# Two of the four sets of activation sums are formed in a later stage of an encoder block, from a second load of x

## The chip, the cores and the metric

One NeuronCore of a Trainium2 chip runs the whole block as one program. The metric is the device time of one execution in microseconds (us); a figure called a median is the median of three runs. A profiled execution has a time of its own and a trace. Its engines are PE (matrix multiply), PEld (the weight loads of PE), ACT (ScalarE), DVE (VectorE), POOL (GpSimd) and SP (which here only issues DMAs). Times "at" a moment are us from the start of the profiled span.

## The reference, cut to what matters

The input x is 512 tokens by 1024 features in float32. One layer is computed:

```python
h = _rmsnorm(x, g_pre_mix)                 # x * rsqrt(mean(x^2) + eps) * g
proj = h @ w_in                            # 1024 x 7168
q, k, v, g, u, sv, a_ret, a_sgu = jnp.split(proj, ...)   # 512,512,1024,1024,1024,1024,1024,1024
y_ret = _retention_branch(q, k, v, g, ret_decay_logit, w_ret_o)
y_sgu = _sgu_branch(u, sv, ..., w_sgu_o)
merged = jax.nn.sigmoid(a_ret) * y_ret + jax.nn.sigmoid(a_sgu) * y_sgu
x = x + _rmsnorm(merged @ w_out, g_post_mix)
h2 = _rmsnorm(x, g_pre_ffn)
x = x + _rmsnorm(_conv_gated_mlp(h2, w_up, conv_w, conv_b, w_down), g_post_ffn)
```

Retention works on chunks of the sequence with learned decays, forward and backward; its output is normed per head, multiplied by silu(g) (the first of the gates) and projected. The spatial branch multiplies gelu(u) by a mix over 128 positions of the normed gelu(sv).

## The kernel before, in words

**Numbers.** Every float32 operand of a matmul is split into a high and a low part in PE's fast float32 form: ACT copies the value into the high part (`copy`, L71) and DVE subtracts it from the value for the low part (`split`, L76 to L78). A product is then three matmuls: high by high, high by low, low by high.

**Weights.** All weight matrices lie in HBM as 146 blocks of 128 by 1024, in the order of use. `w_get` (L154) loads and splits them some blocks ahead: SP issues the load into one of 4 `raw` tiles, ACT and DVE split it into a ring of 9 `w4` slots. A block's split waits until PE is through with the block whose slot it takes, and its load until the split that used the raw tile before is done.

**Order.** The Python code records the work, and when the program is built a scheduler lays it out as one fixed list for each engine. An engine works strictly down its own list; it waits at the head of it when an operand or a buffer isn't ready. SBUF tiles of 128 by 512 come from a pool of 74 (`blk`), short-lived ones from a ring of 6 (`tmp`). PSUM is a ring of 8 banks (`ps`).

**First stage (L188 to L240): q and k.** x is loaded transposed, as eight tiles `xT` of 128 features by 512 tokens. For each k, `load_x` (L190) loads one, ACT multiplies it by the norm's weight into the high part `xh` (L194), DVE makes the low part `xl` (L200), and `x_scaled` (L204) has ACT write the same product once more in plain float32, `xg` (L207). PE then adds this k's part of 8 outputs, which fill all 8 PSUM banks (`qk`). At the end (L317 to L324) ACT copies the four even banks and DVE the four odd ones to SBUF (`qkraw`).

**The sums of activations.** The projections u, a_ret and a_sgu use a seven-product form of a 2 by 2 block multiplication (`Pair`, L600): the two halves of the tokens (T0, T1) by the two halves of the features (k = 0..3 and 4..7). The blocks of x enter as they are and as four sums S1 to S4. `x_forms(k)` (L248) makes one of four sets of those sums from `xg[k]` and `xg[k + 4]`: four DVE operations on half tiles (L252 to L255), and two splits (two ACT copies `sh`, two DVE subtractions `sl`). The four calls stand at L289, behind the sum of squares of x (ACT, L283, on eight more loads of x; DVE, L286; POOL, L273 and L276), which gives the norm's row scale `rstd`.

**Then.** A small matmul spreads `rstd` over a PSUM bank (L329, `rbc`); rotary and decay of head 0 are prepared (`prep`); and six groups `t_group` (L422) of 4 weight blocks each make v (two), sv (two) and g (two), each into 4 banks, with the retention of one head between them. `t_group` yields after each of its 4 blocks. The last group, the second half of g, stands alone at L584; its evacuation `g_evac` (L563) has ACT apply silu into a `tmp` tile, DVE multiply, and PE transpose (L557). u comes next, and its weights come in seven forms (`w_form`, L131): B11, B21 and B22 as loaded, T1 and T3 added by DVE (L142, L143), T2 and T4 added by POOL (L144, L146). Then come the gates with the output projections, `w_out`, and the gated MLP.

Of the kernel before, what the change touches and what calls it, by code (L numbers as in the profile page):

```python
# [12 lines left out]
AF = mybir.ActivationFunctionType  # L13
# [21 lines left out]
PRE, FFNG, LNG, LNB = 0, 8, 16, 24  # L35
# [5 lines left out]
def tile_block(ctx: ExitStack, tc, xT, x, wall, par, cs, decay, wsp, bsp, gpost, gffn, out):  # L41
    nc = tc.nc
# [5 lines left out]
    def nm(s):  # L48
        uid[0] += 1
        return f"{s}_{uid[0]}"  # L50

    def blk(dt=F32, n="blk", shape=(P, S)):
        return sb.tile(list(shape), dt, tag="blk", bufs=NBLK, name=nm(n))

    def tmp(n="tmp", shape=(P, S)):
        return sb.tile(list(shape), F32, tag="tmp", bufs=6, name=nm(n))
# [7 lines left out]
    def ps(shape=(P, S)):  # L64
        return pp.tile(list(shape), F32, tag="ps", name=nm("ps"))
# [4 lines left out]
    def copy(o, i):  # L70
        nc.scalar.activation(out=o, in_=i, func=AF.Copy)  # L71

    def as32(t):
        return t.bitcast(F32)

    def split(hi, lo, src):  # L76
        copy(hi, src)
        nc.vector.tensor_sub(lo, src, as32(hi))  # L78
# [75 lines left out]
    def w_get(look=LOOK):  # L154

        i = w_pos[0]
        w_pos[0] += 1
        room = 2 * look + (2 if units[i][0] == "blk" else 0)
        n = sum(w_size(u) for u in units[i : w_pos[1]])
        while w_pos[1] < len(units) and (w_pos[1] <= i or n + w_size(units[w_pos[1]]) <= max(room, 9 if look == LOOK else 0)):  # L160
            u = units[w_pos[1]]
            w_ready[w_pos[1]] = w_block(u[1]) if u[0] == "blk" else w_form(*u)
            w_pos[1] += 1
            n += w_size(u)
        return w_ready.pop(i)

    def mm3(o, ah, al, bh, bl, start, stop):
        nc.tensor.matmul(o, ah, bh, start=start, stop=False)  # L168
        nc.tensor.matmul(o, ah, bl, start=False, stop=False)  # L169
        nc.tensor.matmul(o, al, bh, start=False, stop=stop)  # L170
# [14 lines left out]
    def col(i):  # L185
        return part[:, i : i + 1]

    xh, xl, xg = [], [], []  # L188

    def load_x(k):  # L190
        t = tmp("xT")
        nc.sync.dma_start(t, xT[k])
        h_, l_ = blk(F32R, "xh"), blk(F32R, "xl")
        nc.scalar.activation(out=h_, in_=t, func=AF.Copy, scale=col(PRE + k))  # L194
        xh.append(h_)
        xl.append(l_)
        return t

    def x_low(k, t):
        nc.vector.scalar_tensor_tensor(  # L200
            out=xl[k], in0=t, scalar=col(PRE + k), in1=as32(xh[k]), op0=ALU.mult, op1=ALU.subtract
        )

    def x_scaled():  # L204
        k = len(xg)
        xg.append(blk(n="xg"))
        nc.scalar.activation(out=xg[k], in_=xts[k], func=AF.Copy, scale=col(PRE + k))  # L207


    hold = raw_tile()  # L210
# [6 lines left out]
    xts = []  # L217
    for k in range(KD):
        xt = load_x(k)
        xts.append(xt)  # L220
        if k:
            x_low(k, xt)
        if k == 2:
            copy(hold[:, 0:16], as32(xl[1])[:, 0:16])
        wh, wl = w_get(1 if k < 4 else LOOK)
        if k == 0:
            x_low(k, xt)
            for a, b in ((wh, xh), (wl, xh), (wh, xl)):
                for m in range(8):
                    nc.tensor.matmul(  # L230
                        qk[m], a[:, m * P : (m + 1) * P], b[0], start=a is wh and b is xh, stop=False
                    )
            continue
        if k > 1:
            x_scaled()
        for m in range(8):
            c = slice(m * P, (m + 1) * P)
            mm3(qk[m], wh[:, c], wl[:, c], xh[k], xl[k], False, k == KD - 1)
    x_scaled()
    x_scaled()  # L240

# [4 lines left out]
    def x_forms(k):  # L248

        a, b = xg[k], xg[k + 4]  # L250
        s_ = blk(n="xs")
        nc.vector.tensor_sub(s_[:, T0], a[:, T1], b[:, T1])  # L252
        nc.vector.tensor_sub(s_[:, T1], s_[:, T0], a[:, T0])
        nc.vector.tensor_sub(a[:, T0], a[:, T0], a[:, T1])
        nc.vector.tensor_add(a[:, T1], b[:, T0], s_[:, T1])  # L255
        for names, s_ in (("S1", "S2"), s_), (("S3", "S4"), a):
            h_, l_ = blk(F32R, "sh"), blk(F32R, "sl")
            split(h_, l_, s_)
            for n, t in zip(names, (T0, T1)):
                forms[n].append((h_[:, t], l_[:, t]))  # L260
# [9 lines left out]
    def rsqrt(o, v, scale, w):  # L270

        t = small("rs", 16, 4)
        nc.gpsimd.tensor_scalar(  # L273
            out=t[:, :w], in0=v, scalar1=scale, scalar2=EPS, op0=ALU.mult, op1=ALU.add
        )
        nc.gpsimd.tensor_tensor(out=o, in0=t[:, :w], in1=nhalf[:, :w], op=ALU.pow)  # L276

    ss = const("ss", [P, 16])
    for t in range(NT):
        for n in range(2):  # L280
# [3 lines left out]
                out=xt, in_=xt, func=AF.Square, accum_out=ss[:, 4 * n + t : 4 * n + t + 1]  # L284
# [1 line left out]
    nc.vector.tensor_add(ss[:, :NT], ss[:, :NT], ss[:, NT : 2 * NT])  # L286
    rstd = const("rstd", [P, NT])
    rsqrt(rstd, ss[:, :NT], 1.0 / D, NT)
    for k in range(4):  # L289
        x_forms(k)  # L290


# [12 lines left out]
    for c in range(19, 1, -2):  # L305
        v.scalar_tensor_tensor(
            out=lc, in0=lc, scalar=1.0 / c, in1=lb, op0=ALU.add, op1=ALU.mult
# [4 lines left out]
        out=lg, in0=lc, scalar=-2.0, in1=lg, op0=ALU.mult, op1=ALU.add  # L312
# [5 lines left out]
    for m in range(8):  # L318
        t = blk(n="qkraw")
# [102 lines left out]
    def t_group():  # L422

        acc = [ps() for _ in range(NT)]
        for kp in range(4):
            wh, wl = w_get()
            for t in range(NT):
                c = slice(t * P, (t + 1) * P)
                for kk in range(2):
                    k = 2 * kp + kk  # L430
                    f = slice(kk * S, (kk + 1) * S)
                    nc.tensor.matmul(acc[t], xh[k][:, c], wh[:, f], start=k == 0, stop=False)  # L432
                    nc.tensor.matmul(acc[t], xh[k][:, c], wl[:, f], start=False, stop=False)  # L433
                    nc.tensor.matmul(acc[t], xl[k][:, c], wh[:, f], start=False, stop=k == KD - 1)  # L434
            yield acc
# [104 lines left out]
    def sv_norm():  # L540
        for t in range(NT):
            for q in range(2):
                z = svz[t, q]
                v.tensor_scalar(
                    out=z, in0=z, scalar1=smv[:, t, 0:1], scalar2=srstd[:, t : t + 1],
                    op0=ALU.subtract, op1=ALU.mult,
                )
# [23 lines left out]
    for h in range(H):  # L571
# [3 lines left out]
        acc = next(gen)  # L575
# [5 lines left out]
        for _ in gen:  # L581
            pass
        (v_evac, sv_evac, sv_evac, g_evac)[h](acc, (1, 0, 1, 0)[h])
    for acc in t_group():  # L584
        pass
    sv_norm()
    g_evac(acc, 1)

# [260 lines left out]
    for t in range(NT):  # L849
        acc = [dn_.finish(t, 0)]  # L850
# [49 lines left out]
    for t in range(NT):  # L900
# [9 lines left out]
        for i, (a, b) in enumerate(((0, 512), (512, 768), (768, 1024)) if t == NT - 1 else ((0, 512), (512, 1024))):  # L910
            v.scalar_tensor_tensor(
                out=z[:, a:b], in0=z[:, a:b], scalar=sc, in1=x1[t][a // S][:, a % S : a % S + b - a],
# [99 lines left out]
```

## Time and profile before

| what | value |
|---|---|
| median of 3 runs | 859.52 us (857.39 to 859.78) |
| the profiled execution's own time | 855.59 us |
| its span in the trace | 853.8 us |
| PE busy | 837.8 us, 98% of the span |
| DVE busy | 547.0 us, 64% |
| ACT busy | 377.8 us, 44% |
| POOL busy | 70.0 us, 8% |
| moved by DMA | 87.88 MB, 103 GB/s on average |

The share of busy time is an average over all stages. Where PE, the busiest engine, stands still, the list of waits says what it waited for, and the timeline when. The "releaser" behind a wait is the instruction whose end let the waiting one go.

### The profile page before, as it was taken

Reading aid. Unit: us, or ns where it says so; the run is one execution under the profiler, and the core shown is the slowest. Engines: PE = TensorE matmul, PEld = TensorE weight load, DVE = VectorE, ACT = ScalarE, POOL = GpSimd, SP = SyncE. Lnnn points to the kernel's source line nnn. Section 1 sums busy time; section 2 is a strip of 40 time slices with the busy share of each in tenths; the row PEclk is TensorE's granted clock in tenths of the full one; section 3 lists DMA queues with packets and bytes.
Section 4 is the critical chain, followed back from the end, with each engine's and each line's share of the span. In section 5 each row is a group of like instructions: output and inputs, shape, how many; then the busy total and the mean of one; then the engine's idle time right before and its main releaser. Section 6 shows DMA issues by size and latency. Waiting matters only on the chain.

```text
span 853.8 us, 11250 instructions
## 1 busy us (share of the span) xinstructions
PE 837.8 (98%) x4444; PEld 722.2 (85%) x4444; DVE 547.0 (64%) x846; ACT 377.8 (44%) x605; POOL 70.0 (8%) x75
## 2 busy tenths in 40 slices
PE   8979999999999999999999999999999999999996
PEld 7858888888899999999988898888888888888885
DVE  5597897865798677767765766666666666322404
ACT  6644446534565444444444564444444444211301
POOL 0010000011131111032210100000000000000000
PEclk9989999999999999999999999999999999999999
DMA  8722121220233333322456033223333333222202
GB/s 280 267 87 99 49 94 58 74 74 25 87 99 125 99 99 99 95 81 97 148 161 259 1 103 100 96 97 99 99 99 98 99 99 99 98 93 92 88 0 99
DMA packets 27126, 87.88 MB, mean 103 GB/s; under 512 B 3073, under 2 KB 3713, under 8 KB 27073
## 3 DMA queue, kind: packets, MB, share of 16 engines
q1 hardware_dynamic: 25776, 84.75, 30.2%
q0 software_dynamic: 432, 1.32, 0.6%
q10 hardware_dynamic: 864, 1.09, 0.4%
q8 instruction: 35, 0.57, 0.3%
q14 instruction: 19, 0.15, 0.1%
HBM read 85.05 MB, written 2.10 MB: 102 GB/s over the span
## 4 chain that ended last, share of the span: by engine, by line
PE 92%; DMA 2%; DVE 2%; ACT 2%; issue 0%; SPq 0%; POOLq 0%; DVEq 0%; ACTq 0%
PE ps L168 14%; PE ps L614 14%; PE ps L169 14%; PE ps L170 14%; PE ps L761 6%; PE ps L760 6%; PE ps L759 6%; PE ps L433 5%; PE ps L432 5%; PE ps L434 5%; DMA raw<-wall 1%; PE ps L684 1%; ACT wh L71 1%; DMA xT<-xT 1%; DVE wl L78 1%; ACT x L283 0%
## 5 line engine op out<-in xcount | busy, mean ns | idle before, releaser
L78 DVE TENSOR_TENSOR wl<-raw,wh 128x1024 fp32r<-128x1024 f32 (+1 forms) x131 | 149.1, 1149 | 159.8 <-PE ps L169 71.2
L71 ACT ACTIVATE wh<-raw 128x1024 fp32r<-128x1024 f32 (+2 forms) x133 | 128.9, 982 | 90.5 <-PE ps L761 45.3
L170 PE MATMUL ps<-h2h,wl 128*128 128x512 f32 (+1 forms) x384 | 142.4, 371 | 0.0
L169 PE MATMUL ps<-h2l,wh 128*128 128x512 f32 (+1 forms) x384 | 142.2, 371 | 0.0
L168 PE MATMUL ps<-h2h,wh 128*128 128x512 f32 (+1 forms) x384 | 142.2, 372 | 0.0
L71 ACT ACTIVATE wf<-raw 128x512 fp32r<-128x512 f32 x84 | 50.9, 627 | 82.0 <-issue 25.8
L78 DVE TENSOR_TENSOR wf<-raw,wf 128x512 fp32r<-128x512 f32 x84 | 66.6, 810 | 27.1 <-ACT wf L71 26.8
L170 PEld LDWEIGHTS ps<-h2h,wl 128*128 128x128 f32 x384 | 72.2, 188 | 12.6
L169 PEld LDWEIGHTS ps<-h2l,wh 128*128 128x128 f32 x384 | 72.3, 188 | 12.5
L168 PEld LDWEIGHTS ps<-h2h,wh 128*128 128x128 f32 x384 | 72.1, 188 | 12.6 <-ACT h2h L825 0.3
L432 PE MATMUL ps<-wh,xh 128*128 128x512 f32 x192 | 75.3, 392 | 0.0
L433 PE MATMUL ps<-wl,xh 128*128 128x512 f32 x192 | 75.1, 391 | 0.0
L434 PE MATMUL ps<-wh,xl 128*128 128x512 f32 x192 | 74.9, 390 | 0.0
L614 PE MATMUL ps<-sh,wf 128*128 128x256 f32 x384 | 73.3, 281 | 0.0
L760 PE MATMUL ps<-wl,fh 128*128 128x512 f32 x176 | 68.5, 389 | 0.0
L761 PE MATMUL ps<-wh,fl 128*128 128x512 f32 x176 | 68.5, 389 | 0.0
L759 PE MATMUL ps<-wh,fh 128*128 128x512 f32 x176 | 68.5, 389 | 0.0
L868 ACT ACTIVATE cv<-ps,part 128x512 f32<-128x512 f32 x44 | 34.3, 780 | 76.0 <-PE ps L170 76.0
L614 PEld LDWEIGHTS ps<-sh,wf 128*128 128x128 f32 x384 | 61.0, 188 | 0.5 <-ACT u L71 0.2
L614 PE MATMUL ps<-xh,wf 128*128 128x256 f32 x288 | 55.3, 282 | 0.0
L614 PE MATMUL ps<-sl,wf 128*128 128x256 f32 x192 | 54.0, 281 | 0.0
L614 PEld LDWEIGHTS ps<-xh,wf 128*128 128x128 f32 x288 | 45.7, 188 | 0.4
(240 smaller groups left out, 1530.0 us busy)
## 6 DMA issues: line engine op xcount, KB each, us to landing
raw<-wall SPq DMA_DIRECT2D x145, 512.0 KB, 3.4
x<-x SPq DMA_DIRECT2D x16, 256.0 KB, 6.0
xT<-xT SPq DMA_DIRECT2D x8, 256.0 KB, 5.3
out<-z SPq DMA_DIRECT2D x4, 256.0 KB, 2.0
out<-z ACTq DMA_DIRECT2D x3, 256.0 KB, 2.0
cs<-cs SPq DMA_DIRECT2D x2, 256.0 KB, 4.0
gpm<-gpost POOLq DMA_DIRECT2D x2, 256.0 KB, 3.7
gpf<-gffn POOLq DMA_DIRECT2D x2, 256.0 KB, 3.5
```

Source lines behind the costliest of these rows:

```text
L71: nc.scalar.activation(out=o, in_=i, func=AF.Copy)
L78: nc.vector.tensor_sub(lo, src, as32(hi))
L168: nc.tensor.matmul(o, ah, bh, start=start, stop=False)
L169: nc.tensor.matmul(o, ah, bl, start=False, stop=False)
L170: nc.tensor.matmul(o, al, bh, start=False, stop=stop)
L432: nc.tensor.matmul(acc[t], xh[k][:, c], wh[:, f], start=k == 0, stop=False)
L433: nc.tensor.matmul(acc[t], xh[k][:, c], wl[:, f], start=False, stop=False)
L434: nc.tensor.matmul(acc[t], xl[k][:, c], wh[:, f], start=False, stop=k == KD - 1)
L614: nc.tensor.matmul(o, w_[:, c], a_, start=first and k == n == 0, stop=k == 3 and n == 2, skip_group_check=True,)
L759: nc.tensor.matmul(o, ah, bh, start=k == 0, stop=False)
L760: nc.tensor.matmul(o, ah, bl, start=False, stop=False)
L761: nc.tensor.matmul(o, al, bh, start=False, stop=k == self.nk - 1)
```

## The change

The sets 0 and 1 stay where they are. For the sets 2 and 3, `xg[2]`, `xg[3]`, `xg[6]` and `xg[7]` are no longer made in the first stage, and `x_forms(2)` and `x_forms(3)` are no longer called at L289. Instead, after the first and after the second weight block of the last `t_group`, two `xT` tiles are loaded again into `tmp` tiles, on POOL's queue; ACT scales them into `xg`, and `x_forms` is called for that set. The arithmetic is the same.

```diff
-    xh, xl, xg = [], [], []
+    xh, xl, xg = [], [], {}
...
-    def x_scaled():
-        k = len(xg)
-        xg.append(blk(n="xg"))
-        nc.scalar.activation(out=xg[k], in_=xts[k], func=AF.Copy, scale=col(PRE + k))
+    def x_scaled(k, t):
+        xg[k] = blk(n="xg")
+        nc.scalar.activation(out=xg[k], in_=t, func=AF.Copy, scale=col(PRE + k))
...
-        if k > 1:
-            x_scaled()
+        if k > 1 and (k - 2) % 4 < 2:
+            x_scaled(k - 2, xts[k - 2])
         for m in range(8):
             c = slice(m * P, (m + 1) * P)
             mm3(qk[m], wh[:, c], wl[:, c], xh[k], xl[k], False, k == KD - 1)
-    x_scaled()
-    x_scaled()
...
-    for k in range(4):
+    for k in range(2):
         x_forms(k)
...
-    for acc in t_group():
-        pass
+    for n, acc in enumerate(t_group()):
+        if n < 2:
+            for k in (n + 2, n + 6):
+                t = tmp("xT")
+                nc.gpsimd.dma_start(t, xT[k])
+                x_scaled(k, t)
+            x_forms(n + 2)
     sv_norm()
     g_evac(acc, 1)
```

## The prediction

> **What bounds the kernel now.** I read PE's waits first, since the page has PE busy for 98% of the span.
>
> ```profile
> PE ps L329 <- ACT qkraw L71: 6.1, 1, 6.1
> PE ps L230 <- ACT wh L71: 1.3, 1, 1.3
> PE ps L216 <- DVE raw L211: 1.0, 1, 1.0
> PE ps L557 <- DVE o L567: 0.3, 1, 0.3
> ```
>
> That is the whole list (total, times, longest): after the start, PE stands still once, for 6.1 us, at L329 between the q/k stage and the first `t_group`, until ACT has emptied a bank into `qkraw`. Everywhere else PE goes from matmul to matmul, so it sets the end: what PE gains there arrives at the end, and other engines' work is free as long as PE doesn't come to wait for it. The timeline of PE around the hole (start, length, what):
>
> ```profile
> 49.36 0.39 PE L170 MATMUL ps<-xh,wl 128*128 128x512 f32 x1
> 55.83 2.05 PE L329 MATMUL ps<-ident,rstd 128*128 128x128 f32 x8 [6.08 <-ACT qkraw L71]
> 57.53 0.77 PE L432 MATMUL ps<-wh,xh 128*128 128x512 f32 x1
> 58.10 0.63 PE L433 MATMUL ps<-wl,xh 128*128 128x512 f32 x1
> 58.53 0.44 PE L434 MATMUL ps<-wh,xl 128*128 128x512 f32 x1
> 58.81 0.39 PE L432 MATMUL ps<-wh,xh 128*128 128x512 f32 x1
> ```
>
> Matmuls start 0.23 us apart before the hole; behind it the first ones are 0.57, 0.43 and 0.28 apart. The windows say why (length, busy time of PE, PEld, DVE, ACT and POOL, then the granted clock):
>
> ```profile
> 50.00:52.00 2.00, 0.00 (x0) 0.00 (x0) 1.81 (x5) 0.55 (x1) 0.00 (x0) 0.95 0.13 51
> 52.00:54.00 2.00, 0.00 (x0) 0.00 (x0) 2.00 (x4) 1.58 (x2) 0.00 (x0) 0.50 0.00 0
> 56.00:58.00 2.00, 2.00 (x9) 2.00 (x10) 2.00 (x4) 1.23 (x4) 0.00 (x0) 0.50 0.75 275
> 58.00:60.00 2.00, 2.00 (x9) 1.55 (x9) 1.97 (x6) 0.71 (x2) 0.00 (x0) 0.84 0.20 16
> ```
>
> PE's clock falls to 0.50 in the hole and stays there for the first 2.8 us of work, while DVE is busy throughout. With what? The timelines of DVE and ACT:
>
> ```profile
> 48.03 0.41 DVE L252 TENSOR_TENSOR xs<-xg,xg 128x256 f32<-128x256 f32 x1
> ...
> 54.06 0.42 DVE L255 TENSOR_TENSOR xg<-xg,xs 128x256 f32<-128x256 f32 x1
> 55.23 0.69 DVE L78 TENSOR_TENSOR sl<-xg,sh 128x512 fp32r<-128x512 f32 x1 [0.76 <-ACT sh L71]
> 55.84 2.48 DVE L321 COPY qkraw<-ps 128x512 f32<-128x512 f32 x4
> ```
> ```profile
> 54.57 0.63 ACT L71 ACTIVATE sh<-xg 128x512 fp32r<-128x512 f32 x1 [0.89 <-DVE xg L255]
> 55.11 2.04 ACT L71 ACTIVATE qkraw<-ps 128x512 f32<-128x512 f32 x4
> ```
>
> From 48.03 on both work on the sets 2 and 3, the ones that are moved, and the copies out of PSUM stand behind them. The banks were full long before: each takes 24 x 0.23 / 8 = 0.68 us in the last k, so bank 0 was complete at about 45.
>
> **What the change takes away at the hole.** On DVE, two calls: 8 half operations and 4 splits, from 48.03 to 55.84, with one weight split (`wl`, 1.22 us at 51.99) among them. On ACT, 4 splits `sh` and 4 scalings `xg` (0.71 us each). In the changed program's lists of instructions PE's list is the same throughout. L329 waits for ACT's copy of bank 0 and for `rstd`; the four banks of the first `t_group` wait for DVE's copy of bank 1, ACT's of 2, DVE's of 3, ACT's of 4. ACT's list there is now: squares of x, `sh` of sets 0 and 1, one weight split, the four copies; DVE's: sets 0 and 1, one `wl`, copies of banks 1, 3 and 5, another `wl` (it needs the stage's last matmuls), bank 7.
>
> I lay them out by the durations of the trace, starting the squares where they start now, at 35.38 (first x tile landed). One square, a weight split, five squares: 40.03, as now. `sh` of set 0 (0.52 from start to start), two squares (0.61 each): 41.8; a weight split 0.95: 42.7; `sh`: 43.3. DVE sums the squares at 41.8, so POOL has `rstd` at about 44 (0.19 + 1.59). DVE's second `sl` of set 0: 43.3 to 43.9; the four halves of set 1 at 0.46: 45.7; two `sl` at 0.6: 46.9; `wl` 1.14: 48.1; copy of bank 1: 48.7. ACT's last `sh` ends at 46.3, a weight split 0.95: 47.25; bank 0: 47.8; bank 2: 48.3.
>
> PE's last matmul of the stage starts at 49.36, so L329 can start at 49.59: bank 0 and `rstd` are there. At full clock its 8 matmuls take half of 57.53 - 55.83 = 1.70, so 0.85, and `t_group` needs bank 1 at 50.44, 1.7 us after it is free. The hole closes, the clock has no reason to fall, and the fourth matmul of `t_group` (58.81 now) starts at 50.44 + 3 x 0.23 = 51.13. The gain is 58.81 - 51.13 = 7.7 us: 55.83 - 49.59 = 6.2 of waiting and 1.4 of half clock.
>
> **What is moved past what there.** On SP the load of the last `xT` goes behind one weight load, so it is issued at 25.6 + 0.4 = 26.0 instead of about 22.7 and lands some 5.3 us later, at 31.3; PE needs its parts at 44.1. ACT waits for it at the head of its list, then has a high part, a weight split and a scaling (0.71 + 1.05 + 0.71) before the first square: 33.8, before the tile of x lands. One weight load of the group after falls behind `cs` on SP; its block isn't used before 90. `cs` itself is issued after `wl` at 48.1 instead of at 53.65, and lands some 4 us later: 52.5, so `prep` of head 0 moves forward about as much as PE (59.70 to 52.5). These cost nothing.
>
> **What it adds in the last group.** Four loads of 256 KB on POOL (issue 0.6 each, as `bst`'s 0.63; that load landed after 3.5 us), 4 scalings (0.62 from start to start) and 4 `sh` (0.55) on ACT: 4.7 us; on DVE 8 halves (0.46) and 4 `sl` (0.6): 6.1 us. They lie, in the new lists, behind the splits `gl` and among the weight splits for u. Times here are those of the run before; all shift together. The cover:
>
> ```profile
> 200.83 2.48 DVE L78 TENSOR_TENSOR gl<-ps,gh 128x512 fp32r<-128x512 f32 x4 [0.45 <-ACT gh L71]
> 205.98 1.29 DVE L78 TENSOR_TENSOR wf<-raw,wf 128x512 fp32r<-128x512 f32 x2 [2.66 <-ACT wf L71]
> 211.48 1.29 DVE L78 TENSOR_TENSOR wf<-raw,wf 128x512 fp32r<-128x512 f32 x2 [4.21 <-ACT wf L71]
> 216.92 1.29 DVE L78 TENSOR_TENSOR wf<-raw,wf 128x512 fp32r<-128x512 f32 x2 [4.15 <-ACT wf L71]
> ```
>
> DVE stands idle for 2.66 + 4.21 + 4.15 = 11.0 us between 203 and 217, ACT for 3.05 + 4.34 + 4.29 = 11.7. All weight splits of the running group are done by 199.1. POOL issues the loads right behind L144 (194.34 + 1.74 = 196.1), its next duty is L146 at 212.25; the two `tmp` tiles of the second pair come free with the multiplications L567 from 195.63 on. First pair landed at about 201, second at about 203; ACT is free for them at 202.3. The weight splits wait for PE to free a slot anyway, and the first is wanted by PE at 224.7, the sums in u's third product at 227.6. So: nothing on PE. Without that cover the 6.1 us on DVE would be the cost.
>
> **Sum.** 855.59 - 7.7 + about 0.2 for hand-overs = 848.1 for a profiled execution. It stands 3.9 under the median of the runs; against that median: 859.52 - 7.5 = 852.0. What the trace can't show: how close PE follows across the seam (0 to 0.4), and when x's tiles land now (up to 1.2 us earlier, since the block's split they queue behind can be; or later, next).
>
> [...] The clock was 1.00 until 51.5 and 0.80 on average from 51.5 to 52.0, so it fell at about 51.8, 2.0 us after the last matmul ended (49.75). [...]
>
> **Rivals.**
> *The hole only shrinks.* The chain through ACT's squares, DVE's set 1 and `wl` must slip 1.7 us before PE notices. x's tiles landing 4 us later than now would do it: bank 1 at 52.7, a hole of 2.3 and, past 2.0, the 1.4 again: gain 4.0, 855.5 against the median. For it: SP's changed order, with one ACT wait in front of the squares. Against: SP issues x's tiles behind the same block's load as before, whose split (29.80 now) doesn't move back.
> *The work moved is felt by u.* POOL's loads land late, ACT stands at `xg` and all behind it. From there to the first silu (217.78) ACT has 4 scalings, 4 `sh`, 6 weight splits and some waits for DVE, about 10 us, so the first pair may land until 207.8, 11.7 us after its issue, unnoticed; the gain is eaten at 19.4 us, and each us more makes the kernel slower: 24 us to landing gives 864. The slowest POOL load of the page took 5.9. [...]
> *No change.* Something else ends the wait at the same time, as `rstd` could; but `rstd` was there at 43.38 + 1.59 = 45.0, ten us before L329 ran.
>
> **Numbers.** Hole closed, 850.5 to 853.5: 0.80. Hole shrinks or the loads cost part, 854 to 857: 0.12. No change: 0.04. Slower: 0.04. The range 849.3 to 856.5 adds the spread of the runs shown (2.1 below their median) at the lower end and the shrinking at the upper. Within 0.3% (2.6 us) is what a measurement here can't tell from nothing: faster 0.91, same 0.05, slower 0.04.
>
> **What the changed profile would show.** No wait at L329 over 0.5 us, the clock 1.00 through 50 to 60, `qkraw` copies on ACT and DVE before 49.6; PE busy about the same, span about 846; no wait of PE between 195 and 230 beyond the 0.3 at L557; DVE's pauses at 203 to 217 filled. I am wrong if x's tiles or the last `xT` land late, or if the list of PE's waits has a new line in u.

## The result and the profile after

The changed kernel takes 849.65 us (median of 4 runs, 847.31 to 854.25); the kernel before, beside it on the same chip, 859.65 (4 runs, 857.39 to 859.78). The ratio is 0.9896 with a 95% interval of 0.9851 to 0.9941: faster by about 10 us (5 to 13 by the interval), where 7.5 were predicted and 852.0 as the time. The profiled execution took 849.06 us, its span 847.3.

The list of PE's waits in the changed kernel, whole (what waits and for what; total, times, longest):

```profile
PE ps L229 <- ACT wh L71: 1.9, 2, 1.3
PE ps L215 <- DVE raw L210: 1.0, 1, 1.0
PE ps L169 <- DVE xl L200: 0.3, 1, 0.3
PE ps L554 <- DVE o L564: 0.3, 1, 0.3
```

The entry of 6.1 us for `qkraw` is gone and none took its place at the seam (the 0.3 at L169 is new and lies at 12.93, in the second k); the last line is the old 0.3 at the transposes of `g_evac` (the functions stand 3 lines higher now, so L557 is L554, L329 is L326, L432 is L429). PE's timeline over the seam between the q/k stage and the first `t_group` (start, length, what):

```profile
50.68 0.39 PE L170 MATMUL ps<-xh,wl 128*128 128x512 f32 x1
50.91 1.05 PE L326 MATMUL ps<-ident,rstd 128*128 128x128 f32 x8
51.72 0.48 PE L429 MATMUL ps<-wh,xh 128*128 128x512 f32 x1
52.03 0.39 PE L430 MATMUL ps<-wl,xh 128*128 128x512 f32 x1
52.27 0.39 PE L431 MATMUL ps<-wh,xl 128*128 128x512 f32 x1
```

The `rstd` matmul starts 0.23 us behind the last q/k matmul, as the q/k matmuls do behind one another, and the projections follow 0.8 us later. The clock in the same stretch (length, busy time of PE, PEld, DVE, ACT and POOL, granted clock, DMA):

```profile
50.00:52.00 2.00, 2.00 (x14) 1.83 (x13) 1.50 (x2) 1.49 (x2) 0.00 (x0) 1.00 0.96 332
52.00:54.00 2.00, 2.00 (x10) 1.62 (x9) 1.97 (x6) 0.86 (x3) 0.00 (x0) 1.00 0.70 207
```

It stays at 1.00. ACT's and DVE's timelines show why PE need not wait, and where the moved work went:

```profile
47.34 1.06 ACT L71 ACTIVATE qkraw<-ps 128x512 f32<-128x512 f32 x2
...
195.81 1.35 ACT L206 ACTIVATE xg<-xT,part 128x512 f32<-128x512 f32 x2
...
200.58 1.32 ACT L206 ACTIVATE xg<-xT,part 128x512 f32<-128x512 f32 x2
```
```profile
48.26 1.28 DVE L318 COPY qkraw<-ps 128x512 f32<-128x512 f32 x2
...
197.19 0.43 DVE L249 TENSOR_TENSOR xs<-xg,xg 128x256 f32<-128x256 f32 x1 [0.20 <-ACT xg L206]
...
204.49 0.69 DVE L78 TENSOR_TENSOR sl<-xg,sh 128x512 fp32r<-128x512 f32 x1 [0.16 <-ACT sh L71]
...
210.60 1.29 DVE L78 TENSOR_TENSOR wf<-raw,wf 128x512 fp32r<-128x512 f32 x2 [4.14 <-ACT wf L71]
```

The copies out of banks 0 and 2 run from 47.34, those of banks 1 and 3 from 48.26: both before the stage's last matmul. The late sums start at 195.81 without a wait for their loads, are done at 205.2, and behind them DVE still has a pause of 4.14 us before the weight splits for u.

To see where each us is, the profiled executions of all kernels are cut at four moments on PE: the first matmul of the second k (the time until then holds what the start of the kernel lost), the last q/k matmul, the 13th matmul of the first `t_group` behind it (in the kernel before the clock is back at 1.00 only at 58.62, between the two), and the first matmul of u. "Split" is when ACT starts to split the second half of the first weight block; all values in us.

| kernel | span | split | 2nd k at | to last q/k | seam | to u | u to end |
|---|---|---|---|---|---|---|---|
| before | 853.8 | 6.04 | 11.45 | 37.91 | 11.51 | 163.87 | 629.06 |
| changed | 847.3 | 6.86 | 12.20 | 38.48 | 3.88 | 163.86 | 628.88 |
| after_again | 852.5 | 9.68 | 17.89 | 37.88 | 3.88 | 163.86 | 628.99 |
| no_late_work | 845.3 | 6.22 | 11.60 | 38.51 | 3.87 | 163.87 | 627.45 |
| forms_late_no_reload | 848.8 | 8.63 | 15.56 | 37.86 | 3.87 | 163.87 | 627.64 |
| one_set_late | 851.0 | 9.41 | 17.46 | 37.86 | 3.87 | 163.87 | 627.94 |
| hole_short | 854.0 | 6.74 | 13.19 | 37.85 | 11.75 | 163.88 | 627.33 |
| hole_long | 859.0 | 6.08 | 11.46 | 38.92 | 17.58 | 163.89 | 627.15 |
| late_twice | 850.8 | 9.48 | 16.44 | 37.85 | 3.87 | 164.26 | 628.38 |
| late_three_times | 861.2 | 8.65 | 16.71 | 37.87 | 3.87 | 163.53 | 639.22 |
| start_by_halves | 847.2 | 6.85 | 11.63 | 39.06 | 3.87 | 163.88 | 628.76 |
| hole_middle | 849.3 | 6.95 | 11.45 | 37.87 | 8.90 | 163.87 | 627.21 |
| before_by_halves | 855.2 | 10.01 | 13.55 | 38.33 | 11.18 | 163.87 | 628.27 |
| start_by_halves_again | 846.4 | 8.15 | 12.16 | 39.07 | 3.87 | 163.87 | 627.43 |

From before to changed the spans differ by 6.5: the seam gives 11.51 - 3.88 = 7.63, the start takes back 0.75 and the q/k stage 0.57 (a late `xl` among it, the wait at L169), the rest adds 0.2. The stretch from the seam to u, in which the late work lies, is 163.86 against 163.87.

### The profile page after: what moved, and what is told of

Same layout as the page of the kernel before. It is cut to its first block, busy times and chain, and to the rows that moved or that the text cites. A ratio compares the mean times of both kernels' runs of the same rounds, so it can differ in the third digit from the quotient of the medians.

```text
span 847.3 us, 11252 instructions
## 1 busy us (share of the span) xinstructions
PE 836.6 (99%) x4444; PEld 721.0 (85%) x4444; DVE 547.2 (65%) x846; ACT 377.9 (45%) x605; POOL 71.5 (8%) x79
## 4 chain that ended last, share of the span: by engine, by line
PE 97%; DMA 1%; DVE 1%; SPq 0%; ACT 0%; issue 0%; POOLq 0%; DVEq 0%; ACTq 0%
PE ps L169 16%; PE ps L168 16%; PE ps L170 15%; PE ps L616 14%; PE ps L763 6%; PE ps L761 6%; PE ps L762 6%; PE ps L429 5%; PE ps L430 5%; PE ps L431 5%; DMA raw<-wall 1%; PE ps L686 1%; PE ps L554 0%; PE ps L823 0%; DVE o L564 0%; PE ps L410 0%
## 5 line engine op out<-in xcount | busy, mean ns | idle before, releaser
L169 PE MATMUL ps<-h2l,wh 128*128 128x512 f32 (+1 forms) x384 | 142.2, 371 | 0.0
L169 PEld LDWEIGHTS ps<-h2l,wh 128*128 128x128 f32 x384 | 72.3, 188 | 12.3
L429 PE MATMUL ps<-wh,xh 128*128 128x512 f32 x192 | 75.0, 391 | 0.0
```

## Experiments: is it the hole, and is the moved work free?

Theory: the change gains what the hole at the seam and the half clock behind it cost (7.6 us), and what it adds is free. Rivals: the gain is partly lower load elsewhere, or the late work costs something that the start's luck hid.

**The changed kernel again**, with nothing edited, for the size of the gain.

> The changed kernel once more, beside the kernel before on the same chip, for a narrower interval. The sum of the prediction (6.2 us of waiting and 1.4 us of half clock at one place) expects 7.5 us less than before, a ratio of 0.991. If the 10.0 us between the medians of the first runs is real, something beyond that place gained 2 to 3 us, and the ratio comes out at 0.988 or below again.

850.8 us (8 runs, 846.22 to 854.27) against 856.32 (13 runs, 853.77 to 861.09): ratio 0.9924 [0.9898, 0.9950]. The ratio is near the 0.991 of the sum and not at 0.988 or below. This time the medians are 5.5 us apart, last time 10.0, and each kernel's runs here spread over 7 us and more. The profiled run of this one is 5.2 us longer than that of the changed kernel in the table, with the same seam and the same time from there to the end; all of it is in the start, which gets its own experiments below.

**The late work left out.**

```diff
-            for k in (n + 2, n + 6):
-                t = tmp("xT")
-                nc.gpsimd.dma_start(t, xT[k])
-                x_scaled(k, t)
-            x_forms(n + 2)
+            for f in forms.values():
+                f.append(f[n])
```

> Leaves out the second load of x, the four scalings and the forming of the sets 2 and 3 altogether (the sets 0 and 1 are used in their place, so the result is not the reference's). If the late work is free, as the sum has it, the time is that of the changed kernel within 0.5 us. If the late work costs PE something that a larger gain elsewhere covers, this is faster than the changed kernel by that cost, up to 6 us.

847.7 us (6 runs, 847.06 to 851.64), ratio 0.9914 [0.9886, 0.9942]. The median is 3.1 us under that of after_again beside it, not within 0.5 as expected, but the intervals overlap, and the runs fall into four at 847 to 848 and two at 851.6. The stretches are sharper. From the seam to u it takes 163.87 us, with the late work 163.86: there the loads, the scalings and the sums cost PE nothing. From u to the end it is 627.45 against 628.88, but hole_middle, with the late work in it, has 627.21 there.

**The sums late, without the second load.** All eight `xg` are made in the first stage as before; the sets 2 and 3 are formed from them in the last group.

```diff
-        if k > 1 and (k - 2) % 4 < 2:
+        if k > 1:
             x_scaled(k - 2, xts[k - 2])
...
+    x_scaled(6, xts[6])
+    x_scaled(7, xts[7])
...
-            for k in (n + 2, n + 6):
-                t = tmp("xT")
-                nc.gpsimd.dma_start(t, xT[k])
-                x_scaled(k, t)
             x_forms(n + 2)
```

> All eight scalings stay in the first stage as before; only the forming of the sets 2 and 3 moves to the last group, without the second load. If DVE's and ACT's work on the sets in front of the copies is the whole cause, this gains as much as the changed kernel (7.5 us, within 1 us), for the four scalings lie in pauses of ACT before the squares. If the scalings or the order of the loads in the first stage matter, it gains clearly less, 3 to 6 us.

851.1 us (848.34 to 852.22), ratio 0.9931 [0.9908, 0.9955], the seam 3.87. The four scalings and the loads are no part of the gain; moving the sums alone closes the hole. The second load saves the room of four tiles over some 150 us, no time.

**Only set 3 late**, set 2 at its old place.

```diff
-        if k > 1 and (k - 2) % 4 < 2:
+        if k > 1 and (k - 2) % 4 < 3:
...
+    x_scaled(6, xts[6])
...
-    for k in range(2):
+    for k in range(3):
         x_forms(k)
...
-        if n < 2:
+        if n == 1:
```

> Only set 3 is moved; set 2 stays in front of the copies. The list of ACT has the copy of bank 0 about 4 us later than in the changed kernel, at 51.7, where PE could use it at 49.6 to 50.9 according to when its first matmul began. Expected: a wait at the row-scale matmul of 0.8 to 2.1 us, no or hardly any half clock, so 5 to 7 us less than before. If the wait were set by something else than this work (the rows' scale, a load of x), there would be no wait at all, or the whole of 6 us.

848.54 us (847.59 to 852.84), ratio 0.9917 [0.9887, 0.9947], and no wait at the seam: the expectation is missed. The profiled run had a late start (the second k at 17.46), so that the last q/k matmul came at 55.32, when ACT, from 53.53 on, had copied three of its four banks; bank 0 was free 1.4 us before it was needed. Whether a hole opens after an early start isn't seen in it; the three runs not profiled (847.59 to 849.0) give no sign of one. Half of the move may do.

**The hole put back, with the change in place.** `rsqrt` is repeated on POOL, so that the matmul behind the seam waits for `rstd`. Nothing else of the change is undone.

```diff
     rsqrt(rstd, ss[:, :NT], 1.0 / D, NT)
+    for _ in range(8):        # hole_long: 11
+        rsqrt(rstd, ss[:, :NT], 1.0 / D, NT)
```

> The changed kernel with the row scale computed 8 times more on POOL, one after the other (about 1.1 us each), so that the row-scale matmul has to wait for it: it is there at about 53, and PE could use it at 49.6 to 50.9. Expected: a hole of 2.3 to 3.6 us. If the clock falls 2.0 us after the last matmul, as in the kernel before, it also pays some 1.4 us at half clock: 3.5 to 5 us slower than the changed kernel. [...]

> The same with 11 repetitions: the row scale is there at about 56.5, a hole of 5.6 to 6.9 us, as long as that of the kernel before, made by another engine and with nothing else changed. If the hole and the clock behind it are the whole difference between the two kernels, this one is as slow as the kernel before (within 1.5 us). If the gain has another source, it stays 2 us or more faster.

A repetition took 1.6 us instead of the 1.1 in the expectations, so both holes are longer than meant. PE's waits, the first line of each list:

```profile
PE ps L328 <- POOL rstd L273: 5.9, 1, 5.9
```
```profile
PE ps L328 <- POOL rstd L273: 11.0, 1, 11.0
```

That makes the first one the better test: its hole of 5.9 us is about that of the kernel before (6.1), in a kernel that has all the rest of the change. It took 858.26 us (10 runs, 855.83 to 863.31) against 858.55 for the kernel before (20 runs): ratio 0.9998 [0.9976, 1.0021], and the seam is 11.75 against 11.51. The hole is thus the whole difference between the kernels, as closely as these runs tell (the interval is some 2 us to either side); with it back, nothing of the gain is left. The long hole: 862.07 us (5 runs, 860.79 to 864.52), ratio 1.0054 [1.0034, 1.0074], seam 17.58. Its median is 3.5 us over the kernel before, though the seam is 6.07 longer: the other stretches scatter too (in the profiled execution 627.15 from u to the end against 629.06), so the medians alone price the hole only to some 2 us.

**The late work done twice, and three times**, with the first results thrown away, to see how much cover there is.

```diff
+            for again in range(2):      # late_three_times: 3
                 for k in (n + 2, n + 6):
                     t = tmp("xT")
                     nc.gpsimd.dma_start(t, xT[k])
                     x_scaled(k, t)
                 x_forms(n + 2)
+                if again < 1:           # 2
+                    for f in forms.values():
+                        f.pop()
```

> The late work done twice (the first result of each set is thrown away): on DVE 12.2 us instead of 6.1, and 11 us of pauses to hold it, on ACT 9.4 in 11.7. By the sum of the prediction the cover is just used up: 0 to 1.5 us slower than the changed kernel. If the late work already costs PE its time, another 3 to 6 us.

> The late work done three times: 18.3 us on DVE, 7 more than the pauses hold, and 14.1 on ACT, 2.4 more. If these pauses were the cover, it is gone now and PE waits in u or at the transposes of the last group: 3 to 7 us slower than the changed kernel. If PE shows no wait, there is more cover than the pauses of that group.

Twice: 852.79 us (850.43 to 853.89), ratio 0.9931 [0.9908, 0.9955]; the stretch to u grows by 0.4 us, to 164.26. Three times: 858.6 us (857.09 to 862.96), ratio 1.0014 [0.9996, 1.0033], so the gain is gone: some 8 us over the changed kernel's two medians, where 3 to 7 were expected. PE's waits there, without the start's:

```profile
PE ps L620 <- ACT sh L71: 3.8, 1, 3.8
...
PE ps L620 <- DVE sl L78: 1.2, 1, 1.2
...
PE ps L554 <- DVE o L564: 1.0, 2, 0.8
PE ps L620 <- DVE gl L78: 0.7, 1, 0.7
```

u (L620 here is its product) waits for the late sums, as the second rival had it. The waits in u sum to 5.7 us, but the stretch from u to the end grows by about 10 (639.22 against 628.88); the windows show the rest:

```profile
227.00:230.00 3.00, 0.48 (x5) 0.28 (x3) 1.19 (x3) 0.63 (x1) 1.86 (x1) 1.00 0.00 0
230.00:233.00 3.00, 0.58 (x1) 0.29 (x1) 2.93 (x5) 1.09 (x2) 1.89 (x2) 0.53 0.04 7
233.00:236.00 3.00, 2.16 (x8) 1.89 (x9) 2.74 (x6) 2.72 (x6) 0.00 (x0) 0.50 0.33 81
236.00:239.00 3.00, 3.00 (x16) 3.00 (x15) 1.77 (x3) 1.38 (x4) 0.00 (x0) 0.50 0.47 175
```

The waits bring the clock down to 0.50 at about 230.2, and PE works at half speed until about 240. The cover holds a little less than twice the late work and not three times.

## Experiments: the start, and the middle of the hole

What the two comparisons left open is why equal seams gave 10.0 and 5.5 us. In the table's columns "split" and "2nd k at", the kernels that keep the old order of the first k fall into two groups: a split at 6.0 to 6.9 us gives a second k at 11.4 to 13.2, one at 8.6 to 9.7 gives 15.6 to 17.9. In after_again, by its list of waits, PE's timeline and the windows:

```profile
PE ps L229 <- ACT wh L71: 3.7, 2, 3.4
```
```profile
5.35 1.57 PE L229 MATMUL ps<-xh,wh 128*128 128x512 f32 x4 [0.29 <-ACT wh L71]
10.36 2.08 PE L229 MATMUL ps<-xh,wh 128*128 128x512 f32 x4 [3.44 <-ACT wh L71]
```
```profile
8.00:10.00 2.00, 0.00 (x0) 0.00 (x0) 0.00 (x0) 0.32 (x1) 0.00 (x0) 0.91 0.91 363
10.00:12.00 2.00, 1.64 (x4) 1.36 (x5) 0.69 (x1) 1.37 (x3) 0.00 (x0) 0.50 0.33 130
```

PE does four matmuls and stands until the second half of the block has landed and been split; in 3.44 us the clock falls too, and the rest of the first k runs at half speed. The load that lands late is the same in both kernels and lies ahead of all that was changed. A second part is when the clock first rises: PE's matmuls in the first k stand 0.43 us apart before that and 0.23 after, and the traces have the rise between 3.8 and 6.6 us in most kernels, but at 9.82 in hole_short, 9.63 in before_by_halves and 12.67 in forms_late_no_reload. If the late landing is most of the spread, more work ahead of the wait should cut it.

```diff
-            for a, b in ((wh, xh), (wl, xh), (wh, xl)):
-                for m in range(8):
+            for half in (range(4), range(4, 8)):
+                for a, b in ((wh, xh), (wl, xh), (wh, xl)):
+                    for m in half:
```

> The changed kernel, with its first k done half by half: the 12 matmuls that need only the first half of the first weight block (columns 0 to 511) come first, then the 12 of the second half; before, 4 came ahead of the first matmul of the second half. Theory (start): the spread of 7 to 8 us between runs of one kernel comes from the landing of the second half of that block (its split on ACT started at 6.0 to 9.7 us), for which PE waits, and where it waits 3.4 us the clock also falls. 8 more matmuls of 0.23 us, 1.8 us, then lie ahead of the wait: an early start (0.6 us of wait) gains up to 0.6 us, a late one (3.4 to 4.5 us of wait) waits 1.6 to 2.7 us, and, if the clock does not fall, saves the 3 us of half clock too. Median 845 to 849 against the changed kernel's 849.7 and 850.8, the slowest runs 2 to 5 us nearer to the fastest, and no change behind the first k (last q/k matmul to 13th v matmul 3.9 us). Rival (not the start): the spread comes from elsewhere; median and spread then stay within 0.5 us of the changed kernel's. Rival (first halves late too): the low parts wl of the first half, or xl, are ready later than the matmuls that now come early; PE then waits for DVE in the first k, and the start gains nothing.

847.86 us (6 runs, 846.71 to 849.51), ratio 0.9896 [0.9872, 0.9920]. The runs lie within 2.8 us where the changed kernel's (after_again) lay within 8.0.

On top of that, five repetitions of `rsqrt` for a hole of middling length:

> The kernel of the run before it in this call, with rsqrt repeated 5 times on POOL ahead of the rb matmul, so that rstd is ready some 8 us (5 times 1.6) later than in the changed kernel, whose POOL had it at about 44 us: at about 52.4 us. The last q/k matmul ends near 50 to 51 us, so a hole of 1 to 3 us stands at the rb matmul after an early start, and none or less after a late one. Theory (the clock falls 2.0 to 2.8 us after the last matmul): a hole under 2 us costs its own length and no clock, so that the stretch from the last q/k matmul to the 13th v matmul is 3.9 us plus the hole, within 0.3; a hole over 2.8 us costs 1 to 1.5 us more at half clock. [...] Time: 1 to 4 us over the run before it.

851.1 us (5 runs, 849.87 to 852.45), ratio 0.9935 [0.9912, 0.9958], 3.2 over the kernel without the hole. The hole in the profile is 3.14 us, and the seam 8.90: 3.87 + 3.14 and 1.9 us of half clock, more than the 1 to 1.5 expected. (The seam is 5.0 us longer than without the hole, the median 3.2: in the profiled executions the q/k stage gives back 1.2 and the stretch behind u 1.5.) The windows at its end:

```profile
52.00:52.50 0.50, 0.00 (x0) 0.00 (x0) 0.00 (x0) 0.00 (x0) 0.50 (x1) 1.00 1.17 389
52.50:53.00 0.50, 0.15 (x1) 0.15 (x2) 0.00 (x0) 0.00 (x0) 0.50 (x2) 0.96 0.96 393
53.00:53.50 0.50, 0.50 (x3) 0.50 (x4) 0.12 (x1) 0.00 (x0) 0.50 (x2) 0.50 0.99 393
```

PE resumed at 52.85, and the clock fell after that, at about 52.96 (0.96 is 0.08 of the half us at 0.50): the rest had ended, and the half clock was paid all the same.

**The change measured without the start's spread**: the kernel before and the changed one, both with the first k by halves, side by side.

> The kernel before, with its first k done half by half as in start_by_halves, and nothing else changed. Theory (the start makes the spread, and the seam makes the change's gain): the runs lie within about 3 us of each other, as start_by_halves did (2.8 us), not 7; the median is 1 to 3 us under that of the kernel before of this call; the stretch from the last q/k matmul to the 13th v matmul stays at 11.5 us; and the median lies 7.0 to 8.3 us over that of start_by_halves_again, closer to the seam's 7.6 than the 10.0 and 5.5 us that the first two comparisons gave. Rival (the change also gains or loses in the start, which the new order hides): the difference to start_by_halves_again is over 9 or under 6.5 us.

> The kernel of start_by_halves again, beside before_by_halves on one chip. Theory (start): spread 2 to 4 us, median 847 to 849; the seam 3.9 us. It is the faster of the two by 7.0 to 8.3 us, which is the change's gain with the start's spread taken out.

Before by halves: 856.1 us (12 runs, 854.92 to 857.44), ratio to the kernel before 0.9980 [0.9967, 0.9994]; changed by halves: 848.18 us (4 runs, 847.27 to 848.93), ratio 0.9887 [0.9868, 0.9905]. Each lies within 2.6 us, the kernel before beside them (17 runs) within 5.3. The difference between the two is 856.1 - 848.18 = 7.9 us, within the 7.0 to 8.3 expected; their seams differ by 11.18 - 3.87 = 7.3, those of the kernels with the old first k by 7.6. The profile of before_by_halves caught the latest landing of all (PE's timeline):

```profile
8.91 1.07 PE L230 MATMUL ps<-xh,wh 128*128 128x512 f32 x4
```
```profile
9.29 1.24 PE L231 MATMUL ps<-xl,wh 128*128 128x512 f32 x4
10.69 1.19 PE L231 MATMUL ps<-xh,wh 128*128 128x512 f32 x4 [0.16 <-ACT wh L71]
```

The first line is start_by_halves, whose second half (split at 6.85) was there in time; the other two are before_by_halves, split at 10.01. Its PE waits 0.16 us instead of 3.44 and begins the second k at 13.55, where after_again, with a split 0.3 us earlier, began it at 17.89. (Its first matmuls stood 0.43 apart, at half clock until 9.63; the windows print 1.00 there only because the trace's record of the clock begins at that rise. That also filled time, and at full speed PE would have waited longer.) The changed kernel by halves has ratios of 0.9896 and 0.9887, without it 0.9896 and 0.9924. The intervals overlap and the two weren't timed side by side, so that it is the faster one isn't shown.

## Why the prediction was right, point by point

- *The hole closes: 6.2 us of waiting and 1.4 of half clock, 7.7, less 0.2 for hand-overs.* Right: 7.63 on the seam, and 7.9 between the two kernels by halves. The 0.2 for hand-overs was not needed; the matmul at L326 follows at 0.23 us. hole_short shows, to some 2 us, that it is the hole and nothing beside it.
- *The order worked out on ACT and DVE: last `sh` done at 46.3, bank 0 copied by 47.8, bank 1 by 48.7, `rstd` at about 44.* Measured: 46.39, about 47.9, about 48.9, 43.98. The 1.7 us to spare were larger, 2.8, since PE came later (bank 1 was needed at 51.72).
- *The late work is free under the pauses before u.* Right: 163.86 against 163.87. The pauses weren't all filled, as the prediction had it: one of 4.14 us is left on DVE. POOL issued the four loads in 2.25 us (0.56 each, estimated 0.6) right behind L144, and they landed after a median of 3.7 us; ACT came to them only after `gh`:

```profile
188.03 1.75 POOL L144 TENSOR_TENSOR raw<-raw,raw 128x512 f32<-128x512 f32 x1 [4.41 <-DVE raw L142]
189.72 2.25 POOL L585 DMA_DIRECT2D xT<-xT  x4
```

- *Rival: the moved work felt by u, through loads that land late.* It did not come about: they landed after a median of 3.7 us, where the rival left the first pair 11.7. POOL's issues, beside DVE's multiplications (L564, 189.31 to 191.7), took 0.56 us each, against the 0.6 of the sum. Where the point lies from which it decides was only half seen: twice the work costs 0.4 us, three times all of the gain.
- *Rival: the hole only shrinks.* No: x's first tile was squared at 35.36, against 35.38 before, as laid out.
- *The time, 852.0 against 849.65.* The step that was off is the reference: I put the gain against the median shown, and took the spread of the three runs as about 2 us. Both kernels spread over 7 to 8 us in the second comparison, for the most part by what happens in the first k, as the kernels by halves show. With that taken out the gain is 7.9, so the 10.0 of the first comparison holds about 2 us of scatter. That the time lies in the stated range is partly luck: 849.65 is under the 850.5 to 853.5 that had the chance of 0.80 for the closed hole, and 0.35 us above the range's lower end, as the median of four runs from 847.31 to 854.25.
- *The profiled time, 848.1 against 849.06; the span, about 846 against 847.3.* The start and the q/k stage took 1.3 us more than in the profile before (0.75 and 0.57), which the change doesn't touch; the seam's 7.63 and 0.2 in the rest do the remainder.
- *The fall of the clock, put at 2.0 us after the last matmul.* From the last matmul's end it took 2.05 us (before), 2.4 (one_set_late's start), 2.6 (hole_long), 2.7 (after_again's start), 2.8 (hole_short), 3.25 (hole_middle) and 5.15 (before_by_halves). So the 2.0 that I read off one profile is no threshold. before_by_halves shows it best, with PE at rest from 52.27 on:

```profile
54.00:56.00 2.00, 0.00 (x0) 0.00 (x0) 2.00 (x4) 1.58 (x2) 0.00 (x0) 1.00 0.00 0
57.00:57.50 0.50, 0.00 (x0) 0.00 (x0) 0.14 (x1) 0.50 (x2) 0.00 (x0) 0.92 1.01 410
```

What these traces share is a grid: the fall and the rise behind it lie whole multiples of 3.41 us apart, 51.80 and 58.62 (before), 54.20 and 61.02 (hole_short), 53.34 and 66.99 (hole_long), 52.96 and 56.38 (hole_middle), 57.42 and 60.83 (before_by_halves). Counted in the stretch of 3.41 us that ends with the fall, PE's rest was 2.05 us (before, 48.39 to 51.80), 2.4 (one_set_late's start), 2.6 (hole_long), 2.7 (after_again's start), 2.8 (hole_short), 3.14 (hole_middle, 49.55 to 52.96) and all 3.41 (before_by_halves, 54.00 to 57.42). Stretches that ended without a fall held 1.26 (before, 4.01 to 7.42) and 1.73 (before_by_halves, 50.59 to 54.00); between 1.73 and 2.05 these traces have nothing. By these numbers what counts is how a rest lies across the grid, and that differs from one execution to the next: a reading of seven falls, which no run was made to test. The shortest hole put in, 3.14 us, paid 1.9 us of half clock.

## What to carry to other kernels

Where an in-order engine feeds a full PSUM at a seam between stages, look at what is queued ahead of the copies: work that isn't due for another 150 us can be moved into a pause that the trace shows, and is free there as long as it fills less than the pause (the 6.1 us on DVE, in pauses of 11.0, cost nothing here; twice that cost 0.4 us, three times that all of the gain). Count a hole on PE with the half clock behind it (1.6 to 2.7 us here, for holes of 3.1 to 11 us), and a pause overfilled in the same way (late_three_times: 5.7 us of waits in u, and 10 us in all). Before a gain of a per cent is read from medians, cut the profiled runs at fixed points of the program: without a hole, the seam and, where the work in it is unchanged, the stretch behind it agree to 0.03 us, where the whole time scatters by 8.

## What was not expected of the hardware

- The load of the second half of the first weight block lands 4.4 us (before) to 8.3 us (before_by_halves) after its issue at 1.6, and is split at 6.0 to 10.0 us, in either kernel. With the wait, the half clock behind it and the moment of the clock's first rise (3.8 to 12.67) this moves everything after it by up to 6.4 us (second k at 11.45 to 17.89). Why it lands so differently wasn't found.
- The clock fell between 2.05 and 5.15 us after the last matmul, on a grid of 3.41 us. In hole_middle it fell about 0.1 us after PE had resumed (at 52.96, PE at 52.85), at the end of the stretch from 49.55 on.
- Half clock after PE resumed cost 1.6 us (before, before_by_halves), 1.9 (hole_middle), 2.0 (hole_short) and 2.7 (hole_long), taken as the seam less 3.87 less the wait.
- From u to the end the executions differ by up to 1.9 us (627.15 to 629.06), without relation to the change; this was not followed up.
